# Order of a channel mixer's wide products, of the next weights' split and of two table transposes in a two-layer encoder trunk

## The chip, the cores and the metric

The kernel runs on one core of a Trainium2 chip. The metric is the device time of one execution in microseconds; the time before is the median of 3 runs. The profile is of one further execution.

The engines are named as in the profile: PE (TensorE's matmuls), PEld (its weight loads), DVE (VectorE), ACT (ScalarE), POOL (GpSimd) and SP (SyncE, which here only issues DMA).

## The reference, cut to what matters

The trunk has two layers over 512 tokens of width 1024. Each has a mixer and a channel mixer.

```python
h = rmsnorm(x, norm_mix_g[l])
proj = h @ a_w_in          # layer 0: queries, keys, values, output gate, 2*4 gate columns, memory queries
...
x = x + concat([mix_out, mem_out]) @ w_out

def conv_ffn(h, w_up, conv_w, conv_b, w_down):     # the channel mixer, D_FF = 2816
    u, g = split(h @ w_up, 2)
    g = causal_dwconv(g, conv_w, conv_b)           # width 3
    return (silu(g) * u) @ w_down
```

All is float32.

## The kernel before, in words

**Arithmetic.** A float32 operand is used as a pair of tiles: a high part, rounded to the type fp32r by ACT (`split`, line 118), and a low part, the remainder, which DVE subtracts (line 119). A product of two pairs is three matmuls (`mm3`, lines 162 to 164): high by high, high by low, low by high. All have 128 partitions and 128 stationary columns; what varies is the number of moving columns, mostly 512 (all tokens) or 256 (half of them). Here a matmul of 512 columns is called wide, one of 256 narrow. Weights come by DMA into `wr` and are split into `wh` and `wl`; each of the three has 3 buffers, the general scratch tile `t` has 8. PSUM tiles have the tags `mm` (3 buffers, `pmm` in the profile), `sc` (3, `psc`) and `tr` (2, `ptr`).

**The channel mixer.** For each of 22 tiles `j` of 128 hidden channels, an up tile and a gate tile are needed. Tiles 5 to 21 (`later`, line 780, one `step`, line 801, for each) take them together as a 2 by 2 block product (up and gate rows; two halves of the contraction; two halves of the tokens) with seven block products in place of eight. A block product of pairs is 12 narrow matmuls (4 contraction tiles by `mm3`; `products`, line 748). Three of the seven (`chain`, line 770, with the weights `s2`, `s3` and `a22`) are added onto the PSUM tile `r1`. In the 12 steps of each layer with `j` in `WIDE` (9 to 20) these three are made by `wide_products` (line 762): the moving tile holds a high part in its first 256 columns and the low part in the other 256, so for each of the 4 contraction tiles one wide matmul (line 767) with the high weights makes high by high and high by low, and one narrow one (line 768) with the low weights makes low by high in the first half. ACT (line 774) then copies the first half out and DVE (line 775) adds the other half.

Between them stand two blocks of the down projection (`down_products`, line 724): 4 contraction tiles by `mm3`, 12 wide matmuls each, into `ptr`. In a WIDE step PE's order is: 24 narrow (two products), the `s2` product, 12 wide (down block 0), 12 narrow, the `s3` product, 12 wide (down block 1), the `a22` product, 12 narrow. PE, ACT and DVE run in the order in which the code is written there (`manual_schedule`).

**The entry.** The first part of layer 0 (`value_columns(1)`, line 971) projects half of the value columns and the gate columns. It loops over 4 pairs of contraction tiles (`u`), each with one weight tile (392 columns) and 24 matmuls. The normalised input tiles are made at the same time: `x_scaled(j)` (DVE line 387, then ACT's cast line 392) and `x_low(j)` (DVE line 395). In the loop's pass `u` the kernel takes the weights that were split before, makes the input tiles `2u+2` and `2u+3`, and only then splits the weights of the next pass (`parts`, lines 118 and 119, pinned: kept in program order). Then come `load_vectors(1)` and `load_vectors(2)` (line 297): each loads a table of 88 rows by SP into a `t` tile (line 302), transposes it on PE into `ptr` (line 305) and copies it on DVE to a constant tile `cols` (line 307). They hold the convolution's coefficients of the two channel mixers. After that `value_columns(0)` and four projections with a convolution (`qk_tile`, line 1083; its accumulator is a `t` tile that ACT first writes at line 1088) and two gate tiles run on PE, woven with `gate_rows` (line 1012), a chain of small DVE and ACT operations that holds six more `t` tiles and sends rows out by DMA from POOL (line 1068, tensor `rowd`). Here a scheduler decides the order on each engine, with the pinned operations kept in theirs.

Of the kernel before, what the change touches and what calls it, by code (L numbers as in the profile page):

```python
# [45 lines left out]
H = S // 2  # L46
# [7 lines left out]
def trunk(  # L54
# [18 lines left out]
    nc = tc.nc  # L73
# [62 lines left out]
    def parts(raw, pinned=False):  # L136
        _, a, b = raw.shape
        hi = sb("wh", [P, D], F32R)[:, : a * b].rearrange("p (a b) -> p a b", a=a)
        lo = sb("wl", [P, D], F32R)[:, : a * b].rearrange("p (a b) -> p a b", a=a)
        split(hi, lo, raw, pinned=pinned)  # L140
        return hi, lo
# [36 lines left out]
    def run(gen):  # L178
        while True:
            try:  # L180
                next(gen)
            except StopIteration as end:
                return end.value

    def chain(*gens):
        for g in gens:
            yield from g
# [109 lines left out]
    def load_vectors(i, stage=None):  # L297
        n = sum(k for _, k in VECS[i])
        at = sum(k for group in VECS[:i] for _, k in group)
        if stage != 1:  # L300
            raw_vectors[i] = sb("t", [P, P])
            nc.sync.dma_start(raw_vectors[i][:n, :], vecs[at : at + n, :])
        if stage != 0:
            tp = ps("tr")
            nc.tensor.transpose(tp[:, :n], raw_vectors[i][:n, :], ident[:n, :n])
            cols = cpool.tile([P, n], F32, name=f"cols{i}")
            V.tensor_copy(cols, tp[:, :n])
            c = 0
            for name, k in VECS[i]:
                col[name] = cols[:, c : c + k]  # L310
                c += k
# [90 lines left out]
    def value_weights(hf, u):  # L402
        n = AW // 2
        ex = rows(a_w_in, 4 * AW, 2 * AH, 2 * u, 2 * u + 2) if hf else None
        return load(rows(a_w_in, 2 * AW + hf * n, n, 2 * u, 2 * u + 2), 2, n, ex)

    with tc.manual_schedule(engines={mybir.EngineType.PE, mybir.EngineType.Activation, mybir.EngineType.DVE}):

        w = ps("mm")
# [53 lines left out]
        vw = [parts(value_weights(1, 0))]  # L463
# [155 lines left out]
    class ChannelMixer:  # L619
# [139 lines left out]

            return [(p[i - 1][:, :H], p[i - 1][:, H:]) for p in self.sums]  # L760

        def wide_products(self, o, w, i):

            n = KT // 2
            for k in range(n):
                both = self.sums[k][i - 1]
                nc.tensor.matmul(o, w[0][:, k], both, start=False, stop=False, skip_group_check=True)  # L767
                nc.tensor.matmul(o[:, :H], w[1][:, k], both[:, :H], start=False, stop=k == n - 1, skip_group_check=True)  # L768

        def chain(self, to, o, w, i, wide):  # L770

            if wide:
                self.wide_products(o, w, i)
                A.copy(to, o[:, :H])  # L774
                V.tensor_tensor(out=to, in0=to, in1=o[:, H:], op=ALU.add)  # L775
            else:
                self.products(o, w, self.t(i))
                A.copy(to, o[:, :H])
# [22 lines left out]
        def step(self, j, w, nxt, tail):  # L801
            def then(o, *names):
                for name in names if o is not None else ():
                    getattr(o, name)()

            new = Tail(self, j)
            then(tail, "last_block", "first_tap")
            w.split_fourth()
            r1, r2, new.r3 = ps("mm"), ps("mm"), ps("sc")
            new.up, new.u3, new.pre = sb("t", [P, S]), sb("t", [P, S]), sb("t", [P, S])  # L810
            self.products(r1, w.a11, self.b(0, 0), True)
            A.copy(new.up[:, :H], r1[:, :H])
            then(tail, "second_tap")
            self.products(r2, w.a12, self.b(1, 0), True)
            V.tensor_tensor(out=new.up[:, :H], in0=new.up[:, :H], in1=r2[:, :H], op=ALU.add)
            then(tail, "third_tap")
            wide = j in WIDE
            self.chain(new.up[:, H:], r1, w.s2, 2, wide)
            then(nxt, "sums")
            then(tail, "gated")  # L820
            then(nxt, "split_second", "sum_third")
            w.down_products(0)
            self.products(new.r3, w.s1, self.t(1), True)
            w.add_down(0)
            then(tail, "split")
            then(nxt, "split_up")
            self.chain(new.u3[:, :H], r1, w.s3, 3, wide)
            V.tensor_tensor(out=new.pre[:, H:], in0=new.u3[:, :H], in1=new.r3[:, :H], op=ALU.add)
            then(nxt, "split_sums")
            w.down_products(1)  # L830
            then(nxt, "sum_fourth")
            w.add_down(1)
            self.chain(new.pre[:, :H], r1, w.a22, 4, wide)
            then(nxt, "split_down", "split_gate")
            self.products(new.r3, w.s4, self.b(1, 1))
            return new, nxt
# [134 lines left out]
    def value_columns(hf):  # L971
        n = AW // 2
        os_ = [ps(t) for t in ("mm", "mm", "mm", "sc")]
        for u in range(4):
            if hf:

                wh, wl = vw.pop()
                for j in range(2 * u + 2, min(2 * u + 4, KT)):
                    if j < KT - 1:
                        x_scaled(j + 1)  # L980
                    x_low(j)
                if u < 3:
                    vw.append(parts(value_weights(1, u + 1), pinned=True))
            else:
                wh, wl = parts(value_weights(0, u))
            nn = wh.shape[-1]
            for i in range(2):
                k = 2 * u + i
                for T in range(TT):
                    lh, ll = (t[:, T * P : (T + 1) * P] for t in act[k])  # L990
                    mm3(os_[T][:, :nn], lh, ll, wh[:, i, :], wl[:, i, :], k == 0, k == KT - 1)
                    yield
        for T in range(TT):
            if hf:
                V.tensor_add(gt[:, T, :], os_[T][:, n : n + 8], gateb)
            hi, lo = sb("u", [P, S], F32R), sb("u", [P, S], F32R)
            G.memset(f(hi)[:, DH : DH + P], 1.0)
            G.memset(f(lo)[:, DH : DH + P], 0.0)
            split(pair(hi), pair(lo), os_[T][:, :n].rearrange("p (a b) -> p a b", a=2))
            vh[hf][T], vl[hf][T] = hi, lo  # L1000
# [3 lines left out]
    e, u, c, r = (cpool.tile([P, TT, AH], F32, name=f"gate{i}") for i in range(4))  # L1004
# [224 lines left out]

    outp = OutProjection(a_w_out, mixes, (0, 3, "mm"), (3, 5, "sc"))  # L1230
    run(value_columns(1))
    load_vectors(1)
    load_vectors(2)
    for j in range(KT):
        pin(G.dma_start(xspill[j], xT[j]))
    fill = gate_rows()
    weave(chain(value_columns(0), a_tiles(0, 1)), fill, 0.3)
    run(fill)
    for s in range(TT):
        exponents(0, s)  # L1240
    for s in range(TT):
# [42 lines left out]
    for j in range(KT):  # L1284
        wh, wl = weights(rows(ffn_w_down[0], j * P, P, FT - LAST, FT), LAST, P)
        o = ps("mm")
# [174 lines left out]
    n = LAST // 2  # L1461
    for hf in range(2):
# [6 lines left out]
        for Ts, pieces in groups:  # L1469
            for c in pieces:  # L1470
                if c.start:
                    os_[Ts[0]] = ps("mm")
                for u in range(n):
# [3 lines left out]
                    wh, wl = ws[u]  # L1477
                    for T in Ts:
                        for i in range(2):
                            k = 2 * u + i  # L1480
# [58 lines left out]
```

## Time and profile before

| | us |
|---|---|
| median of 3 runs | 1193.16 (1192.63 to 1193.5) |
| the profiled execution, its own time | 1192.82 |
| its span | 1191.0 |
| PE busy | 1179.6 |
| DVE busy | 960.3 |
| ACT busy | 731.6 |

Matmuls are pipelined, so each one's duration in the trace (about 0.39 us wide, 0.28 us narrow) overlaps the next one's. What a matmul costs is the distance from its start to the next start, which the timeline shows. In the timeline a row is: start, duration, engine, line, operation, out<-in, shape, and in brackets the idle time before it and what ended it. For a matmul, `pmm<-u,wh` names the moving tile and then the stationary one or the other way round, as the kernel passes them.

### The profile page before, as it was taken

Reading aid. Unit: us, or ns where it says so; the run is one execution under the profiler, and the core shown is the slowest. Engines: PE = TensorE matmul, PEld = TensorE weight load, DVE = VectorE, ACT = ScalarE, POOL = GpSimd, SP = SyncE. Lnnn points to the kernel's source line nnn. Section 1 sums busy time; section 2 is a strip of 40 time slices with the busy share of each in tenths; the row PEclk is TensorE's granted clock in tenths of the full one; section 3 lists DMA queues with packets and bytes.
Section 4 is the critical chain, followed back from the end, with each engine's and each line's share of the span. In section 5 each row is a group of like instructions: output and inputs, shape, how many; then the busy total and the mean of one; then the engine's idle time right before and its main releaser. Section 6 shows DMA issues by size and latency. Waiting matters only on the chain.

```text
span 1191.0 us, 18093 instructions
## 1 busy us (share of the span) xinstructions
PE 1179.6 (99%) x6651; PEld 1029.0 (86%) x6651; DVE 960.3 (81%) x1720; ACT 731.6 (61%) x1299; POOL 145.7 (12%) x234
## 2 busy tenths in 40 slices
PE   9999999999999999999999999999999999999997
PEld 9988888888899889888888888888889988888986
DVE  6877788888878888888788888987896888888855
ACT  4547788766656555555576667775665655555545
POOL 0203102011021111101020000101101011111100
PEclk9999999999999999999999999999999999999999
DMA  8636422457475776665563223244746565665451
GB/s 280 203 107 154 105 75 71 140 172 171 97 174 139 166 165 159 162 141 116 157 214 106 80 71 96 71 135 152 185 100 131 135 138 127 141 142 141 118 158 71
DMA packets 208746, 162.80 MB, mean 137 GB/s; under 512 B 8484, under 2 KB 188170, under 8 KB 208658
## 3 DMA queue, kind: packets, MB, share of 16 engines
q1 hardware_dynamic: 186450, 120.78, 35.1%
q0 software_dynamic: 22208, 40.87, 17.4%
q8 instruction: 52, 0.85, 0.3%
q14 instruction: 36, 0.29, 0.1%
HBM read 133.09 MB, written 32.47 MB: 139 GB/s over the span
## 4 chain that ended last, share of the span: by engine, by line
PE 93%; DVE 3%; ACT 2%; issue 1%; DVEq 0%; ACTq 0%
PE pmm L162 15%; PE pmm L163 15%; PE pmm L164 15%; PE pmm L767 6%; PE ptr L162 6%; PE psc L164 6%; PE ptr L164 6%; PE psc L163 6%; PE ptr L163 6%; PE psc L162 6%; PE pmm L768 3%; PE psc L499 2%; PE ptr L1366 1%; PE ptr L1387 1%; PE ptr L1388 1%
## 5 line engine op out<-in xcount | busy, mean ns | idle before, releaser
L162 PE MATMUL pmm<-u,wh 128*128 128x512 f32 (+1 forms) x872 | 307.9, 353 | 0.1
L163 PE MATMUL pmm<-u,wh 128*128 128x512 f32 (+1 forms) x872 | 306.3, 351 | 0.5 <-DVE u L119 0.5
L164 PE MATMUL pmm<-u,wl 128*128 128x512 f32 (+1 forms) x872 | 306.2, 352 | 0.0
L119 DVE TENSOR_TENSOR wl<-wr,wh 128x1024 fp32r<-128x1024 f32 (+4 forms) x172 | 195.0, 1136 | 63.6 <-ACT wh L118 61.8
L118 ACT CAST wh<-wr 128x1024 fp32r<-128x1024 f32 (+4 forms) x172 | 168.4, 981 | 94.9 <-PE pmm L163 35.6
L164 PEld LDWEIGHTS pmm<-u,wl 128*128 128x128 f32 x872 | 165.1, 189 | 20.8
L163 PEld LDWEIGHTS pmm<-u,wh 128*128 128x128 f32 x872 | 165.4, 190 | 19.2 <-DVE u L119 1.1
L162 PEld LDWEIGHTS pmm<-u,wh 128*128 128x128 f32 x872 | 165.2, 190 | 18.7 <-ACT u L118 0.5
L735 POOL DMA_DIRECT2D xspill<-t x64 | 56.2, 878 | 398.7 <-ACT t L734 389.8
L162 PE MATMUL ptr<-u,wh 128*128 128x512 f32 x256 | 101.3, 396 | 0.0
L164 PE MATMUL ptr<-u,wl 128*128 128x512 f32 x256 | 100.4, 392 | 0.0
L163 PE MATMUL ptr<-u,wh 128*128 128x512 f32 x256 | 100.0, 391 | 0.0
L118 ACT CAST u<-pt 128x512 fp32r<-128x512 f32 x102 | 62.8, 618 | 45.9 <-DVE pt L865 45.8
L162 PE MATMUL psc<-u,wh 128*128 128x256 f32 (+1 forms) x248 | 82.4, 332 | 0.0
L163 PE MATMUL psc<-u,wh 128*128 128x256 f32 (+1 forms) x248 | 82.1, 331 | 0.0
L119 DVE TENSOR_TENSOR u<-pt,u 128x512 fp32r<-128x512 f32 x102 | 70.0, 687 | 5.8 <-ACT u L118 2.4
L928 ACT ACTIVATE t<-t 128x512 f32<-128x512 f32 x34 | 21.5, 633 | 78.9 <-DVE t L639 78.9
L767 PE MATMUL pmm<-u,u 128*128 128x512 f32 x192 | 69.7, 397 | 0.0
L775 DVE TENSOR_TENSOR t<-t,pmm 128x256 f32<-128x256 f32 x72 | 30.1, 418 | 47.2 <-ACT t L774 47.2
L734 ACT COPY t<-ptr 128x512 f32<-128x512 f32 x64 | 37.4, 585 | 45.0 <-PE ptr L164 45.0
L164 PE MATMUL psc<-u,wl 128*128 128x256 f32 (+1 forms) x200 | 63.5, 318 | 0.0
L639 DVE SCALAR_TENSOR_TENSOR t<-t,cols,t 128x511 f32<-128x511 f32 x80 | 59.5, 744 | 3.7 <-ACT t L646 3.7
(299 smaller groups left out, 2698.2 us busy)
## 6 DMA issues: line engine op xcount, KB each, us to landing
wr<-in_ffn_w_up_dram SPq DMA_DIRECT2D x54, 512.0 KB, 4.2
pt<-in_ffn_w_up_dram SPq DMA_DIRECT2D x34, 512.0 KB, 5.8
wr<-in_ffn_w_down_dram SPq DMA_DIRECT2D x34, 512.0 KB, 4.0
xspill<-t POOLq DMA_DIRECT2D x64, 256.0 KB, 5.0
wr<-in_a_w_in_dram SPq DMA_DIRECT2D x20, 512.0 KB, 3.8
xspill<-u POOLq DMA_DIRECT2D x32, 256.0 KB, 2.8
u<-xspill SPq DMA_DIRECT2D x32, 256.0 KB, 5.3
wr<-in_w_kv_dram SPq DMA_DIRECT2D x12, 512.0 KB, 3.7
```

The costliest lines, as they stand in the source:

```text
L118: high = A.copy(hi, src) if on_act else V.tensor_copy(hi, src)
L119: low = V.tensor_tensor(out=lo, in0=src, in1=f(hi), op=ALU.subtract)
L162: nc.tensor.matmul(o, lh, rh, start=first, stop=False, skip_group_check=more)
L163: nc.tensor.matmul(o, lh, rl, start=False, stop=False, skip_group_check=more)
L164: nc.tensor.matmul(o, ll, rh, start=False, stop=last, skip_group_check=more)
L499: nc.tensor.matmul(o, a, b, start=first and i == 0, stop=i == 1)
L639: V.scalar_tensor_tensor(acc[:, n:], src[:, : S - n], self.fw[:, c * FT + j : c * FT + j + 1], acc[:, n:], op0=ALU.mult, op1=ALU.add,)
L734: A.copy(t, o)
L735: G.dma_start(xspill[j], t, accum_op=ALU.add)
L767: nc.tensor.matmul(o, w[0][:, k], both, start=False, stop=False, skip_group_check=True)
L768: nc.tensor.matmul(o[:, :H], w[1][:, k], both[:, :H], start=False, stop=k == n - 1, skip_group_check=True)
L775: V.tensor_tensor(out=to, in0=to, in1=o[:, H:], op=ALU.add)
```

## The change

It has three parts.

1. In `wide_products` the eight matmuls of a product no longer alternate. Before down blocks 0 and 1 (`s2`, `s3`) the four narrow ones come first and the four wide ones after them, next to the block; in `a22`, behind down block 1, the four wide ones come first (`after=True`).
2. In `value_columns(1)` the split of the next pass's weights stands between the two input tiles of a pass, not behind both.
3. The two tables of `load_vectors` are loaded where they were, but transposed and copied only after the gate rows.

```diff
-        def wide_products(self, o, w, i):
+        def wide_products(self, o, w, i, after=False):
 
             n = KT // 2
-            for k in range(n):
-                both = self.sums[k][i - 1]
-                nc.tensor.matmul(o, w[0][:, k], both, start=False, stop=False, skip_group_check=True)
-                nc.tensor.matmul(o[:, :H], w[1][:, k], both[:, :H], start=False, stop=k == n - 1, skip_group_check=True)
-
-        def chain(self, to, o, w, i, wide):
+            halves = [p[i - 1] for p in self.sums]
+            jobs = [(o[:, :H], w[1][:, k], halves[k][:, :H]) for k in range(n)]
+            both = [(o, w[0][:, k], halves[k]) for k in range(n)]
+            jobs = both + jobs if after else jobs + both
+            for k, (to, lh, rh) in enumerate(jobs):
+                nc.tensor.matmul(to, lh, rh, start=False, stop=k == 2 * n - 1, skip_group_check=True)
+
+        def chain(self, to, o, w, i, wide, after=False):
 
             if wide:
-                self.wide_products(o, w, i)
+                self.wide_products(o, w, i, after)
...
-            self.chain(new.pre[:, :H], r1, w.a22, 4, wide)
+            self.chain(new.pre[:, :H], r1, w.a22, 4, wide, True)
...
         for u in range(4):
             if hf:
 
-                wh, wl = vw.pop()
+                wh, wl = vw.pop(0)
                 for j in range(2 * u + 2, min(2 * u + 4, KT)):
                     if j < KT - 1:
                         x_scaled(j + 1)
                     x_low(j)
-                if u < 3:
-                    vw.append(parts(value_weights(1, u + 1), pinned=True))
+                    if u < 3 and j == 2 * u + 2:
+                        vw.append(parts(value_weights(1, u + 1), pinned=True))
...
     run(value_columns(1))
-    load_vectors(1)
-    load_vectors(2)
+    load_vectors(1, 0)
+    load_vectors(2, 0)
...
     run(fill)
+    load_vectors(1, 1)
+    load_vectors(2, 1)
```

On PE, in a WIDE step, from the `s2` product to the first matmul of down block 0, before (the number behind a name is the tile's own; `u_3206`, `u_3260`, `u_3318` and `u_3372` are the moving tiles of the four contraction tiles, `u_4021` and `u_4022` the high and low weights):

```order
L767 MATMUL pmm_4129<-u_3206,u_4021 128x512
L768 MATMUL pmm_4129<-u_3206,u_4022 128x256
L767 MATMUL pmm_4129<-u_3260,u_4021 128x512
L768 MATMUL pmm_4129<-u_3260,u_4022 128x256
L767 MATMUL pmm_4129<-u_3318,u_4021 128x512
L768 MATMUL pmm_4129<-u_3318,u_4022 128x256
L767 MATMUL pmm_4129<-u_3372,u_4021 128x512
L768 MATMUL pmm_4129<-u_3372,u_4022 128x256
L162 MATMUL ptr_4182<-u_3382,wh_4094 128x512
```

The same place of the changed kernel, where the one call stands at line 770:

```order
L770 MATMUL pmm_4129<-u_3206,u_4022 128x256
L770 MATMUL pmm_4129<-u_3260,u_4022 128x256
L770 MATMUL pmm_4129<-u_3318,u_4022 128x256
L770 MATMUL pmm_4129<-u_3372,u_4022 128x256
L770 MATMUL pmm_4129<-u_3206,u_4021 128x512
L770 MATMUL pmm_4129<-u_3260,u_4021 128x512
L770 MATMUL pmm_4129<-u_3318,u_4021 128x512
L770 MATMUL pmm_4129<-u_3372,u_4021 128x512
L162 MATMUL ptr_4182<-u_3382,wh_4094 128x512
```

The same eight matmuls run, but the changes between 512 and 256 columns are fewer. The `s3` product moves in the same way; in `a22` the four wide ones follow down block 1 directly and the four narrow ones stand ahead of the 12 narrow ones of the step's last product. A WIDE step then has runs of 44 narrow (12 of the step before, 24, 4 of `a22` and 4 of `s2`), 16 wide, 16 narrow and 20 wide matmuls.

On DVE, in passes 0 and 1 of `value_columns(1)`, before (`wl_603` and `wl_646` are the low weights of passes 1 and 2, the rows of L387 and L395 the input tiles):

```order
L395 TENSOR_TENSOR u_537<-t_534,u_536 128x512
L387 SCALAR_TENSOR_TENSOR t_593<-u_454,cols_521,rb_517 128x512
L395 TENSOR_TENSOR u_590<-t_587,u_589 128x512
L119 TENSOR_TENSOR wl_603<-wr_599,wh_602 128x784
L387 SCALAR_TENSOR_TENSOR t_630<-u_461,cols_521,rb_517 128x512
L395 TENSOR_TENSOR u_596<-t_593,u_595 128x512
L387 SCALAR_TENSOR_TENSOR t_636<-u_468,cols_521,rb_517 128x512
L395 TENSOR_TENSOR u_633<-t_630,u_632 128x512
L119 TENSOR_TENSOR wl_646<-wr_642,wh_645 128x784
```

The same stretch of the changed kernel (`wl_597` and `wl_640` are the low weights of passes 1 and 2 there):

```order
L395 TENSOR_TENSOR u_537<-t_534,u_536 128x512
L119 TENSOR_TENSOR wl_597<-wr_593,wh_596 128x784
L387 SCALAR_TENSOR_TENSOR t_600<-u_454,cols_521,rb_517 128x512
L395 TENSOR_TENSOR u_590<-t_587,u_589 128x512
L387 SCALAR_TENSOR_TENSOR t_630<-u_461,cols_521,rb_517 128x512
L395 TENSOR_TENSOR u_603<-t_600,u_602 128x512
L119 TENSOR_TENSOR wl_640<-wr_636,wh_639 128x784
L387 SCALAR_TENSOR_TENSOR t_643<-u_468,cols_521,rb_517 128x512
L395 TENSOR_TENSOR u_633<-t_630,u_632 128x512
```

Each weight split has moved two rows forward, past one L387 and one L395. On ACT the cast of the high weights has moved ahead of one cast of an input tile in the same way (`wh_596` now follows `u_589` directly).

On PE, in the last pass of `value_columns(1)`, the changed kernel (`wh_682` and `wl_683` are that pass's weights, `psc_778` and `wh_781` belong to `value_columns(0)`, which follows):

```order
L162 MATMUL pmm_583<-wh_682,u_645 128x392
L162 MATMUL pmm_584<-wh_682,u_645 128x392
L162 MATMUL pmm_585<-wh_682,u_645 128x392
L162 MATMUL psc_586<-wh_682,u_645 128x392
L162 MATMUL psc_778<-wh_781,u_525 128x384
L163 MATMUL pmm_583<-wl_683,u_645 128x392
L164 MATMUL pmm_583<-wh_682,u_646 128x392
```

Before, the scheduler had put no matmul of `value_columns(0)` ahead of the end of `value_columns(1)`; now one matmul with the next weights stands 20 rows ahead of it. Behind the pass the two matmuls of line 305 stood before; they now follow the last matmul of the two gate tiles.

## The prediction

> **What bounds the kernel now.** I read the page first, for the share of each engine and the granted clock.
>
> ```profile
> span 1191.0 us, 18093 instructions
> PE 1179.6 (99%) x6651; PEld 1029.0 (86%) x6651; DVE 960.3 (81%) x1720; ACT 731.6 (61%) x1299; POOL 145.7 (12%) x234
> PEclk9999999999999999999999999999999999999999
> PE 93%; DVE 3%; ACT 2%; issue 1%; DVEq 0%; ACTq 0%
> ```
>
> PE is busy all the time at an even clock and carries 93% of the chain that ended last. So time comes only from PE: a wait of PE that goes, or matmuls that start closer together. The view of PE's waits, its longest row:
>
> ```profile
> PE pmm L162 <- ACT wh L118: 1.4, 1, 1.4
> ```
>
> It is one wait of 1.4 us in a span of 1191. What else is to be had stands in the distance between starts, and that I read from PE's timeline. First, wide matmuls in a long run without narrow ones (layer 0's channel mixer, before the WIDE steps), and then one block of 12 wide ones that stands between long runs of narrow ones, with the first WIDE step behind 48 narrow ones:
>
> ```profile
> 299.51 0.39 PE L164 MATMUL psc<-u,pt 128*128 128x512 f32 x1
> 299.74 0.39 PE L162 MATMUL psc<-u,wh 128*128 128x512 f32 x1
> 299.96 0.39 PE L163 MATMUL psc<-u,wh 128*128 128x512 f32 x1
> 300.19 0.39 PE L164 MATMUL psc<-u,pt 128*128 128x512 f32 x1
> ...
> 382.11 0.40 PE L162 MATMUL ptr<-u,wh 128*128 128x512 f32 x1
> ...
> 384.86 0.28 PE L162 MATMUL pmm<-u,u 128*128 128x256 f32 x1
> ```
>
> The long run takes 0.68 us for three, 0.227 us a wide matmul. The block of 12 takes 384.86 - 382.11 = 2.75 us, 0.03 us more than 12 x 0.227 = 2.72: that is what one entry from narrow to wide costs when clean runs meet. Now one WIDE step, from its `s2` product to the next one's:
>
> ```profile
> 390.61 0.40 PE L767 MATMUL pmm<-u,u 128*128 128x512 f32 x1
> ...
> 396.24 0.40 PE L767 MATMUL pmm<-u,wh 128*128 128x512 f32 x1
> ...
> 397.65 0.40 PE L162 MATMUL ptr<-u,wh 128*128 128x512 f32 x1
> ...
> 400.43 0.39 PE L767 MATMUL pmm<-u,u 128*128 128x512 f32 x1
> ...
> 401.83 0.28 PE L162 MATMUL psc<-u,u 128*128 128x256 f32 x1
> ...
> 406.15 0.40 PE L767 MATMUL pmm<-u,u 128*128 128x512 f32 x1
> ```
>
> The step takes 406.15 - 390.61 = 15.54 us, with no idle bracket in it. The 48 narrow ones from 384.86 to 390.61 give 5.75 / 48 = 0.120 us a narrow matmul. By these two paces the `s3` product (396.24 to 397.65, four of each) would take 4 x (0.227 + 0.120) = 1.39; it takes 1.41. The block behind it (to 400.43) takes 2.78 in place of 2.72. So where 512 and 256 columns alternate, the starts are a little further apart, and the block behind them pays too.
>
> **Part 1, the wide products.** Nothing is added or removed on any engine; the order on PE changes, and the runs become 44 narrow, 16 wide, 16 narrow, 20 wide: 60 narrow x 0.1198 = 7.19 us, 36 wide x 0.2267 = 8.16, and two entries of 0.03: 15.41 us. Against 15.54 that is 0.13 us a step. How many steps:
>
> ```profile
> L767 PE MATMUL pmm<-u,u 128*128 128x512 f32 x192 | 69.7, 397 | 0.0
> L767 PE MATMUL pmm<-u,wh 128*128 128x512 f32 x96 | 34.9, 398 | 0.0
> ```
>
> 192 + 96 = 288 wide matmuls at 12 a step are 24 steps: 24 x 0.13 = 3.1 us. The bounds: with no cost at all for an entry 15.35, 0.19 a step, 4.6 us; if each of the two entries keeps what the block behind an alternation pays now (2.78 - 2.72 = 0.06), 15.47, 0.07 a step, 1.7 us. I take the middle one, since its row is a block of the same tiles between clean runs.
>
> Here a rule of the Trainium skill speaks against the change. The trace has 0.227 us and 0.120 us in clean runs and 2.78 us for a block whose clean price is 2.72. The page "TensorE: Matmul & The Clock Gate", section "Back-to-back issue gap", gives the distance of warm matmuls as the moving columns over 2.4 GHz plus 2.5 ns, by the number of columns alone, whatever stands before. By it this part would be worth nothing, since the same matmuls run. Worked out as an estimate it gives 0.216 and 0.109 us; the trace doesn't agree, in both paces and in that the same 12 matmuls take 2.75 or 2.78.
>
> What hides the change from the other engines: each product ends as far ahead of the next block as before, as the last wide one starts 0.23 us ahead of it and lasts 0.40, where the last narrow one starts 0.12 ahead and lasts 0.28. The first matmul of `a22` writes `r1`, which ACT and DVE must have read after `s3`:
>
> ```profile
> 397.85 0.37 ACT L774 COPY t<-pmm 128x256 f32<-128x256 f32 x1 [0.22 <-PE pmm L768]
> 398.80 0.41 DVE L775 TENSOR_TENSOR t<-t,pmm 128x256 f32<-128x256 f32 x1
> ```
>
> DVE has read it at 399.21, and `a22` starts at 400.43: 1.22 us to spare, of which the shorter block takes some 0.05.
>
> **Part 2, the weights' split at the entry.** Here PE, ACT, DVE and SP around the wait of 1.44 us:
>
> ```profile
> 40.19 0.34 PE L164 MATMUL pmm<-wh,u 128*128 128x392 f32 x1
> 41.96 0.80 PE L162 MATMUL pmm<-wh,u 128*128 128x392 f32 x3 [1.44 <-ACT wh L118]
> ...
> 52.92 0.34 PE L164 MATMUL psc<-wh,u 128*128 128x392 f32 x1
> ...
> 55.05 0.34 PE L164 MATMUL psc<-wh,u 128*128 128x392 f32 x1
> 55.23 0.32 PE L305 MATMUL ptr<-ident,t 88*128 88x88 f32 x2
> 55.34 0.42 PE L162 MATMUL pmm<-wh,u 128*128 128x384 f32 x1
> ```
>
> ```profile
> 37.36 1.28 ACT L392 CAST u<-t 128x512 fp32r<-128x512 f32 x2 [0.76 <-DVE t L387]
> 40.55 0.62 ACT L392 CAST u<-t 128x512 fp32r<-128x512 f32 x1 [1.90 <-DVE t L387]
> 41.07 0.84 ACT L118 CAST wh<-wr 128x784 fp32r<-128x784 f32 x1
> ```
>
> ```profile
> 39.17 0.68 DVE L395 TENSOR_TENSOR u<-t,u 128x512 fp32r<-128x512 f32 x1
> 39.77 0.74 DVE L387 SCALAR_TENSOR_TENSOR t<-u,cols,rb 128x512 f32<-128x512 f32 x1
> 40.43 0.68 DVE L395 TENSOR_TENSOR u<-t,u 128x512 fp32r<-128x512 f32 x1
> 41.94 0.97 DVE L119 TENSOR_TENSOR wl<-wr,wh 128x784 fp32r<-128x784 f32 x1 [0.83 <-ACT wh L118]
> ```
>
> ```profile
> 29.38 0.37 SPq L131 DMA_DIRECT2D wr<-in_a_w_in_dram x1
> 42.95 0.37 SPq L131 DMA_DIRECT2D wr<-in_a_w_in_dram x1
> wr<-in_a_w_in_dram SPq DMA_DIRECT2D x7, 384.0 KB, 4.6
> ```
>
> PE needs pass 1's high weights at 40.19 + 0.18 = 40.37 and gets them at 41.96, because ACT's cast at 41.07 stands behind the cast at 40.55, and that behind DVE's L387 at 39.77. In the new order ACT can cast them behind the two casts of 37.36, from 38.6 to 39.4; they were issued at 29.38, and the median transfer takes 4.6 us. DVE takes the low part at 39.77, done at 40.7; PE needs it four matmuls into the pass, at 41.1. The wait goes: 41.96 - 40.37 = 1.59 us.
>
> After the wait the 72 matmuls of passes 1 to 3 take 55.23 - 41.96 = 13.27 us. Their pace at the end is (55.05 - 52.92) / 12 = 0.1775, which would make 12.78; 0.49 us go to small gaps behind the wait, with the low weights arriving late. So the most that this part can bring is 1.59 + 0.49 = 2.1 us (2.3 with the rounding of the steps). What is late next: the input tiles, which the split now stands ahead of. I rolled DVE and ACT on with the starts above (L387 0.66 to the next, L395 0.60, the split 0.90 to 0.97, and between them the wait for ACT's cast). DVE then ends the low weights of passes 2 and 3 at about 45.1 and 49.4, and PE, with 24 x 0.1775 = 4.26 us a pass, needs them at 45.3 and 49.7; the second input tile of pass 1 is needed at 42.8 and ready at 42.1. All are met, with 0.2 to 0.7 us to spare. I take 2.1 us; if the two short margins fail by half a microsecond each, 1.1 us are left.
>
> The matmul with `wh_781` that now stands 20 rows ahead of the end of the last pass is a new wait, behind which all of PE's matmuls queue. Its weights are asked for when DVE has split pass 1's (before: 41.94 + 0.97, and SP at 42.95; now about 40.75), land 4.6 us later at 45.4 and are cast behind pass 3's at about 49.2. PE gets there at 49.6.
>
> **Part 3, the tables.** The two transposes take 55.34 - 55.23 = 0.11 us where they are and as much where they go, so they cost nothing; the two copies on DVE move too, and no step of PE waits for them. What is new is that two of the eight `t` tiles stay taken while the gate rows hold six. By the order's list of waits, the second convolution's accumulator on ACT now waits for the first two `rowd` transfers, whose tile it takes over:
>
> ```profile
> 82.70 0.52 POOL L1068 DMA_DIRECT2D rowd<-t  x1 [5.22 <-DVE t L1066]
> rowd<-t POOLq DMA_DIRECT2D x1, 6.0 KB, 1.7
> 85.10 0.76 ACT L1088 ACTIVATE t<-pmm,cols 128x512 f32<-128x512 f32 x1
> ```
>
> The second transfer lands at 84.4, 0.7 us ahead of ACT's step at 85.10, and all of this moves forward together with PE. Behind that step ACT queues casts of weights that PE uses microseconds later. I take nothing, and up to 0.2 us either way.
>
> **The sum.** 3.1 + 2.1 = 5.2 us. The profiled execution took 1192.82, which becomes 1187.6. The median of the runs shown is 0.34 above it: 1188.0.
>
> **The rivals.** First, order doesn't matter: the distances in the alternation come from something that stays (the tiles of the product, or PSUM). Then only the entry pays: 1193.16 - 2.1 = 1191.1. Against it speaks that a block of 12 wide ones, the same in both places, takes 2.75 behind narrow ones and 2.78 behind an alternation. The rule of the Trainium skill's page "TensorE: Matmul & The Clock Gate" named above would end here. Second, the entry gives nothing: another weight or input tile is as late as the one repaired, and PE waits as long a little later: 1193.16 - 3.1 = 1190.1. For it speaks that the margins above are 0.2 to 0.7 us and worked out by hand. Third, slower: the matmul with `wh_781` blocks PE. It is the only place where the change puts a wait in front of work that could run. Each microsecond by which its cast ends after 49.6 costs one; after 5.2 all that was won is gone, and after 7.6 the kernel is 2.4 us slower, 1195.6. The transfer would then have to take some 15 us where the median takes 4.6.
>
> **How the numbers follow.** A measurement of this kernel can tell about 0.2%, 2.4 us, from no change; faster therefore means below 1190.8. The forecast, both parts with their bounds, has a chance of 0.80; the entry giving nothing 0.08, which is still faster; order not mattering 0.09, which counts as the same; the blocked PE 0.03. So faster 0.88, the same 0.09, slower 0.03. The range takes the bounds: 4.6 + 2.3 = 6.9 below 1193.16 is 1186.3, and 1.7 + 1.1 = 2.8 below it is 1190.4. It holds the second rival and leaves out the first and the third.
>
> **What would show it.** A WIDE step of 15.41 us from `s2` to `s2` in place of 15.54, and blocks of 12 between wide ones in place of the alternation at 0.227 us each, show part 1; a step of 15.54 refutes it. No idle bracket of PE near 40.4 and the matmul that stands at 55.34 now starting near 53.2 show part 2. A bracket on the matmul of `value_columns(0)` near 49.6, on ACT's L1090 near 83, or on the first matmul of `a22`, would show the waits that I hold to be covered. A time above 1190.4 or below 1186.3 would show a price that I have not seen.

## The result, and the profile after

| | before | after |
|---|---|---|
| median of the runs taken together on one chip | 1193.51 us (1192.63 to 1195.81, 6 runs) | 1188.69 us (1188.06 to 1190.78, 6 runs) |
| ratio, 95% interval | | 0.9961, 0.9949 to 0.9973 |
| the profiled execution and its span | 1192.82 us, 1191.0 us | 1188.06 us, 1186.1 us |

The changed kernel is 4.8 us faster; the interval holds 3.2 to 6.1 us. The forecast was 1188.0 with a range of 1186.3 to 1190.4. One of the seven executions of an experiment below (the wide products alone) took 1943.39 us at a granted clock of 0.56, and its ratio leaves that one out. The page of the changed kernel begins like this (span, busy time of the engines, granted clock, chain of waits by engine):

```profile
span 1186.1 us, 18067 instructions
PE 1175.6 (99%) x6651; PEld 1030.1 (87%) x6651; DVE 960.2 (81%) x1720; ACT 731.5 (62%) x1299; POOL 144.6 (12%) x234
PEclk9999999999999999999999999999999999999999
PE 94%; DVE 2%; ACT 2%; issue 1%; DMA 0%; ACTq 0%; DVEq 0%
```

PE still bounds all, with the same number of matmuls. One WIDE step of the changed kernel on PE's timeline, where the view joins matmuls of one line into groups (x8 is four of 256 columns and four of 512):

```profile
389.31 1.57 PE L770 MATMUL pmm<-u,u 128*128 128x256 f32 x8
...
394.87 0.64 PE L770 MATMUL pmm<-u,wl 128*128 128x256 f32 x4
395.35 1.09 PE L770 MATMUL pmm<-u,wh 128*128 128x512 f32 x4
...
399.01 1.54 PE L770 MATMUL pmm<-u,u 128*128 128x512 f32 x8
...
404.71 1.57 PE L770 MATMUL pmm<-u,u 128*128 128x256 f32 x8
```

From `s2` to `s2` it is 404.71 - 389.31 = 15.40 us, where it was 15.54. Now the entry, first PE at the old wait and at the end of the last value pass, with the matmul with `wh_781` as the second of the row at 49.53, and then ACT's step near 83 that the prediction named:

```profile
40.29 0.34 PE L164 MATMUL pmm<-wh,u 128*128 128x392 f32 x1
40.47 0.69 PE L162 MATMUL pmm<-wh,u 128*128 128x392 f32 x3
...
49.53 0.51 PE L162 MATMUL psc<-wh,u 128*128 128x392 f32 x2
...
53.25 0.34 PE L164 MATMUL psc<-wh,u 128*128 128x392 f32 x1
54.26 0.41 PE L162 MATMUL pmm<-wh,u 128*128 128x384 f32 x1 [0.67 <-DVE gt L997]
```

```profile
83.77 0.76 ACT L1090 ACTIVATE t<-pmm,cols 128x512 f32<-128x512 f32 x1
```

The wait of 1.44 us at 40.4 is gone, and the two rows that might have become waits carry no bracket. But the next product's first matmul, which could have started at 53.25 + 0.18 = 53.43, starts at 54.26, behind a wait that the kernel before doesn't have. What holds it is seen on SP, ACT and DVE:

```profile
40.86 4.71 SPq L131 DMA_DIRECT2D wr<-in_a_w_in_dram  x2
```

```profile
51.10 0.84 ACT L118 CAST wh<-wr 128x768 fp32r<-128x768 f32 x1 [1.87 <-DMA wr<-in_a_w_in_dram]
53.04 0.86 ACT L118 CAST u<-pmm 128x384 fp32r<-128x384 f32 x2 [1.10 <-DVE gt L997]
```

```profile
48.53 1.84 DVE L119 TENSOR_TENSOR wl<-wr,wh 128x784 fp32r<-128x784 f32 x2
51.98 0.96 DVE L119 TENSOR_TENSOR wl<-wr,wh 128x768 fp32r<-128x768 f32 x1 [1.60 <-ACT wh L118]
52.85 0.23 DVE L997 TENSOR_TENSOR gt<-pmm,gateb 128x8 f32<-128x8 f32 x2
53.56 0.56 DVE L119 TENSOR_TENSOR u<-pmm,u 128x384 fp32r<-128x384 f32 x1 [0.47 <-ACT u L118]
```

Read it from below. PE's `pmm` bank is free when DVE has taken the low part of the first eviction (53.56 + 0.56 = 54.12; the bracket of PE names the gate addition, of which one ends at about the same time). That needs ACT's cast at 53.04, that the gate addition at 52.85, and this stands in DVE's order behind the split of 51.98. The split is of the second next weights: the second of SP's pair, issued at about 45.2 and landed by 51.1, when ACT casts them. DVE waits 1.60 us for weights that PE uses only near 57.6, while a bank that PE uses at 53.43 is kept full.

Where the 4.9 us between the last matmuls of the two profiled executions lie, counted by the k-th matmul of each on PE (differences to the kernel before in us, minus where it is earlier; the entry is the stretch from 22 to 108 us, which holds the tables' two transposes in either place, and its first half ends at 45 us; the WIDE steps are all 24, elsewhere is the rest). Below this count is called the ledger:

| kernel | first 22 us | entry, its first half and second half | WIDE steps | elsewhere | all |
|---|---|---|---|---|---|
| after | +0.10 | -2.01 +0.81 | -3.36 | -0.49 | -4.94 |
| after, measured again | 0.00 | -2.00 +0.67 | -3.36 | +0.41 | -4.28 |

So the entry gives 2.0 us and loses 0.7 to 0.8 of it again. What lies elsewhere is mostly not the change's: it is 0.49 us less in one profile and 0.41 us more in the other of the same kernel.

### The profile page after: what moved, and what is told of

It is laid out like the page before. It is cut to its first block, busy times and chain, and to the rows that moved or that the text cites. A ratio compares the mean times of both kernels' runs of the same rounds, so it can differ in the third digit from the quotient of the medians.

```text
span 1186.1 us, 18067 instructions
## 1 busy us (share of the span) xinstructions
PE 1175.6 (99%) x6651; PEld 1030.1 (87%) x6651; DVE 960.2 (81%) x1720; ACT 731.5 (62%) x1299; POOL 144.6 (12%) x234
## 4 chain that ended last, share of the span: by engine, by line
PE 94%; DVE 2%; ACT 2%; issue 1%; DMA 0%; ACTq 0%; DVEq 0%
PE pmm L162 15%; PE pmm L164 15%; PE pmm L163 15%; PE pmm L770 8%; PE ptr L162 6%; PE ptr L163 6%; PE ptr L164 5%; PE psc L164 5%; PE psc L163 5%; PE psc L162 5%; PE psc L499 2%; PE ptr L1370 1%; PE ptr L582 1%; PE ptr L1391 1%; PE ptr L1392 1%; PE ptr L568 1%
## 5 line engine op out<-in xcount | busy, mean ns | idle before, releaser
L770 PE MATMUL pmm<-u,u 128*128 128x256 f32 (+1 forms) x384 | 74.7, 337 | 0.0
L770 PEld LDWEIGHTS pmm<-u,u 128*128 128x128 f32 x384 | 60.7, 190 | 7.8
```

The costliest lines, as they stand in the source:

```text
L770: nc.tensor.matmul(to, lh, rh, start=False, stop=k == 2 * n - 1, skip_group_check=True)
```

## The experiments

The first four kernels were timed together. Three leave parts of the change out, one turns the grouping round.

**The wide products alone** (the kernel before, with the new `wide_products`, `chain` and the call for `a22`):

> The kernel before with the grouped wide products alone. Theory (each switch from 256 to 512 columns costs PE time, and grouping leaves 2 of 13 switches a step): a WIDE step takes 15.40 us from `s2` to `s2` in place of 15.54, 24 x 0.14 = 3.4 us, so the time is 3.2 to 3.6 us below the kernel before. The wait of 1.4 us near 40.4 us stays. Rival (the gain after the change came from the entry and from chance, and order doesn't matter): within 0.5 us of the kernel before.

1190.06 us against 1192.90 for the kernel before, 2.8 us less by the medians; ratio 0.9971, 0.9959 to 0.9983, which is 3.5 us less, between 2.0 and 4.9. In the ledger the WIDE steps give 3.36 us and all of it 3.31; the old wait stands (PE's longest wait):

```profile
PE pmm L162 <- ACT wh L118: 1.4, 1, 1.4
```

Order matters, and the prediction's first rival falls.

**The entry alone** (the kernel before with the split and the tables, WIDE steps as before):

> The kernel before with the weights' split at the entry and the tables alone; WIDE steps as before. Theory (the wait near 40.4 us goes, but the second next weights land late, hold DVE ahead of the gate additions and so PE for 0.7 to 0.9 us near 54): 1.0 to 1.5 us below the kernel before, with a bracket of about 0.7 us on the first matmul of the next product near 54.3 us. Rival, the prediction's sum: 2.1 us below and no such bracket. In both a WIDE step stays at 15.54 us.

1192.99 us, ratio 0.9996, 0.9987 to 1.0005: between 1.6 us less and 0.6 more, which can't be told from nothing. The 1.0 to 1.5 us that I had expected are not seen in the time. PE at the start of the next product:

```profile
55.52 0.34 PE L164 MATMUL psc<-wh,u 128*128 128x392 f32 x1
56.68 0.41 PE L162 MATMUL pmm<-wh,u 128*128 128x384 f32 x1 [0.82 <-DVE gt L995]
```

The bracket is there, as expected. In the ledger its entry gives 2.00 us and loses 0.98, net 1.02. That the profiled execution is none the less slower than the kernel before (1194.47) comes from another place, long before the first instruction that the change moves:

```profile
7.11 1.11 PE L422 MATMUL psc<-ident,u 128*128 128x128 f32 x4 [0.98 <-DMA u<-in_mem_dram]
```

PE waits here for the first loads, and behind it matmuls of 256 columns start 0.21 us apart until 10.4 us, although the granted clock reads 1.00 there. Other profiles wait 1.1 and 1.2 us at the same place and go on at the usual pace; what slows this one isn't shown. The first 22 us of this profile are 2.36 us longer than before's; over all profiles they vary from -0.27 to +2.36. The entry's gain of 1.02 us is smaller than this variation.

**Grouped, but on the far side** (the changed kernel with one line turned round):

```diff
-            jobs = both + jobs if after else jobs + both
+            jobs = jobs + both if after else both + jobs
```

> The changed kernel with the wide products still grouped, but on the far side: ahead of the narrow ones in `s2` and `s3`, behind them in `a22`. A step then enters 5 runs of wide matmuls in place of 2 (13 before). Theory (an entry behind a long narrow run costs 0.02 to 0.026 us net): 15.46 to 15.48 us a step, 1.4 to 1.9 us above the changed kernel. Rival 1 (each of the 11 switches saved is worth the same 0.013 us): 15.44 us, 0.9 us above. Rival 2 (only the strict alternation costs, the neighbour block doesn't matter): 15.40 us, the same time as the changed kernel.

1190.91 us, ratio 0.9982, 0.9973 to 0.9991. One step from `s2` to `s2` on PE's timeline:

```profile
390.42 1.56 PE L770 MATMUL pmm<-u,u 128*128 128x512 f32 x8
...
405.89 1.56 PE L770 MATMUL pmm<-u,u 128*128 128x512 f32 x8
```

15.47 us, as the theory of the price of an entry had it; the WIDE steps give 1.60 us where the changed kernel's give 3.36. Of these two orders, standing together alone brings half of the gain, and standing beside the block as well brings the other half.

**The split without the tables' move** (against the entry alone):

```diff
-    load_vectors(1, 0)
-    load_vectors(2, 0)
+    load_vectors(1)
+    load_vectors(2)
...
-    load_vectors(1, 1)
-    load_vectors(2, 1)
```

> The kernel before with the weights' split at the entry, and the two tables where they stood, in front of the next product. Theory (the tables cost nothing in either place): within 0.2 us of the kernel with entry and tables. Rival: the tables' transposes and copies stand between the last value product and the next on PE and DVE, just where the evictions are late now, and add 0.1 to 0.5 us.

1194.72 us, ratio 1.0014, 1.0005 to 1.0022, single runs from 1192.73 to 1197.56: slower than the kernel before, and 1.7 us above the entry alone, more than either theory had. PE, and then the busy time, the granted clock (the column behind POOL's) and the busy share of the DMA engines (behind the clock) in stretches:

```profile
49.87 0.34 PE L162 MATMUL psc<-wh,u 128*128 128x392 f32 x1
53.02 0.58 PE L305 MATMUL ptr<-ident,t 88*128 88x88 f32 x2 [2.81 <-DMA t<-in_vecs_dram]
53.32 0.68 PE L163 MATMUL pmm<-wl,u 128*128 128x392 f32 x1
53.79 0.53 PE L164 MATMUL pmm<-wh,u 128*128 128x392 f32 x1
54.12 0.53 PE L163 MATMUL pmm<-wl,u 128*128 128x392 f32 x1
```

```profile
49.00:50.00 1.00, 1.00 (x7) 0.88 (x5) 1.00 (x2) 0.57 (x1) 0.00 (x0) 1.00 1.02 362
50.00:53.00 3.00, 0.21 (x2) 0.01 (x1) 0.72 (x1) 0.83 (x1) 0.00 (x0) 0.88 1.00 332
53.00:54.00 1.00, 0.98 (x4) 0.98 (x5) 0.56 (x3) 0.00 (x0) 0.00 (x0) 0.50 0.86 315
...
58.00:59.00 1.00, 1.00 (x4) 1.00 (x4) 0.64 (x3) 0.48 (x1) 0.00 (x0) 0.50 0.01 1
59.00:60.00 1.00, 1.00 (x7) 1.00 (x7) 0.79 (x4) 0.16 (x1) 0.00 (x0) 0.95 0.00 0
```

The tables aren't where they stood. With the new split, the scheduler puts their two transposes into the last value pass, 20 matmuls ahead of its end, where their transfer isn't there yet: PE waits 2.81 us. Then the clock is granted at 0.50 for 6 us, and matmuls that started 0.178 us apart start 0.328 apart (54.12 - 53.79 = 0.33): 16 of them at 0.15 more and one at 0.30 make 2.7 us. The ledger has 5.83 us lost behind the old wait.

**The changed kernel again, and three repairs of the new wait**, timed together.

> The changed kernel once more, on a chip together with the next three. Theory (the two parts simply add, and the entry nets 0.3 to 1.1 us of its 2 us): 3.4 + 0.7 = 4.1 us below the kernel before, 3.7 to 4.6. Rival (the parts help each other beyond their sum, or the first measurement's 4.8 us is the steady value): 4.8 us or more.

1188.67 us (1188.29 to 1189.58), ratio 0.9963, 0.9951 to 0.9976: 4.7 us less by the medians. That lies between the two theories, and the interval holds both, so the timing doesn't decide. The ledger (above) speaks for the sum of the two parts: the WIDE steps give the same 3.36 us here as alone, and the entry 1.33, a little more than the 1.1 that I had allowed; 0.41 us are lost elsewhere.

The writes of `xspill` later:

```diff
-    for j in range(KT):
-        pin(G.dma_start(xspill[j], xT[j]))
     fill = gate_rows()
-    weave(chain(value_columns(0), a_tiles(0, 1)), fill, 0.3)
+
+    def spills():
+        for j in range(KT):
+            pin(G.dma_start(xspill[j], xT[j]))
+        yield from ()
+
+    weave(chain(value_columns(0), spills(), a_tiles(0, 1)), fill, 0.3)
```

> The changed kernel with the eight writes of `xspill` issued behind the next value product, not ahead of it. Theory (these writes share the DMA with the second next weights, whose late landing holds DVE ahead of the gate additions): the weights land about 4 us after their issue at 45.2, near 49.5 and not 51.1, the bracket on the first matmul of the next product (0.7 us) goes, and the time is 0.8 us below the changed kernel. Rival (the chain of addition, cast and subtraction behind the last value matmul is itself too long): the bracket stays at 0.3 us or more, and the gain is under 0.4 us.

1189.17 us (1188.35 to 1189.36), ratio 0.9963, 0.995 to 0.9977: no gain in the time. ACT's cast of the second weights, and PE at the start of the next product:

```profile
51.52 0.84 ACT L118 CAST wh<-wr 128x768 fp32r<-128x768 f32 x1 [1.21 <-DMA wr<-in_a_w_in_dram]
```

```profile
54.32 0.34 PE L164 MATMUL psc<-wh,u 128*128 128x392 f32 x1
54.68 0.41 PE L162 MATMUL pmm<-wh,u 128*128 128x384 f32 x1
```

The weights land 2.80 us ahead of the last value matmul (54.32 - 51.52), where the changed kernel has 53.25 - 51.10 = 2.15: 0.65 us earlier, not the 1.6 that I had expected. The 0.65 are enough to shrink the wait from 54.26 - 53.43 = 0.83 to 54.68 - 54.50 = 0.18. But the edit did less than its text says. POOL's issues of the writes, first in the changed kernel and then here:

```profile
41.87 4.26 POOL L1237 DMA_DIRECT2D xspill<-u  x8
```

```profile
44.14 4.28 POOL L1240 DMA_DIRECT2D xspill<-u  x8
```

The first 22 us of this profile are 1.07 us longer, so the scheduler issues the writes only 1.2 us later (44.14 - 41.87 - 1.07), still around the second weights' issue and not behind the next value product. What the transfer would take without them is not shown. In the ledger the entry is 1.82 us below the kernel before, 0.5 to 0.6 better than the changed kernel's, and the first 22 us of this profile give 1.16 back.

The evictions ahead of the second weights:

```diff
-                wh, wl = parts(value_weights(0, u))
+                wh, wl = vn.pop(0) if vn else parts(value_weights(0, u))
...
+        if hf:
+            vn.append(parts(value_weights(0, 0)))
         for T in range(TT):
+            if hf and T == 3:
+                vn.append(parts(value_weights(0, 1), pinned=True))
             if hf:
-                V.tensor_add(gt[:, T, :], os_[T][:, n : n + 8], gateb)
+                pin(V.tensor_add(gt[:, T, :], os_[T][:, n : n + 8], gateb))
...
-            split(pair(hi), pair(lo), os_[T][:, :n].rearrange("p (a b) -> p a b", a=2))
+            split(pair(hi), pair(lo), os_[T][:, :n].rearrange("p (a b) -> p a b", a=2), pinned=hf == 1)
```

> The changed kernel with the second next weights split behind the first three evictions on ACT and DVE, in program order, and the writes of `xspill` where they are, so that the late landing stays but holds nothing. Theory (the wait is one of order in DVE's queue): the transfer still lands near 51, the bracket near 54.3 goes, 0.8 us below the changed kernel. Rival (the evictions are themselves the limit, or the second weights are then late for PE near 57.6): the bracket stays, or a new one stands near 57.6; gain under 0.4 us or a loss.

1188.26 us (1188.10 to 1188.47), ratio 0.9958, 0.9946 to 0.9971. ACT and PE:

```profile
54.75 0.48 ACT L118 CAST u<-pmm 128x384 fp32r<-128x384 f32 x1 [0.70 <-DVE gt L1003]
55.13 1.57 ACT L118 CAST wh<-wr 128x768 fp32r<-128x768 f32 x2
```

```profile
53.42 0.34 PE L164 MATMUL psc<-wh,u 128*128 128x392 f32 x1
53.62 0.41 PE L162 MATMUL pmm<-wh,u 128*128 128x384 f32 x1
```

The transfer and the writes are untouched, the second weights are cast 4 us later than in the changed kernel, and the wait is gone. This is the clean test: it was the order in DVE's queue. (The edit changes ACT's order too, but in the changed kernel ACT stood idle for 1.10 us ahead of its first eviction, waiting for DVE.) In the ledger the entry gives 1.84 us net, 0.5 to 0.6 more than the changed kernel's. By the times it is 0.4 us, which is inside both spreads.

Both edits together:

> Both edits: the writes later, and the three evictions ahead of the second weights. Theory: either edit alone takes the whole wait, so both together are worth 0.8 us, not 1.6, and the spread from run to run is smaller than the changed kernel's. Rival (each takes a part of it): more than either alone by 0.3 us or more.

1188.22 us (1187.36 to 1189.47), ratio 0.9958, 0.9946 to 0.9971; the entry gives 1.83 net, the same as either edit alone. They remove the same wait. The spread, which I had expected to shrink, didn't; the first 22 us of this profile alone take 1.18 us more than before's.

**Three more**, on the steps that were still open. The wide products in twos:

```diff
-            jobs = both + jobs if after else jobs + both
+            first, second = (both, jobs) if after else (jobs, both)
+            jobs = first[:2] + second[:2] + first[2:] + second[2:]
```

> The changed kernel with the wide products in twos: two narrow, two wide, two narrow, two wide in `s2` and `s3`, and in `a22` two wide, two narrow, two wide, two narrow. A step enters 5 runs of wide matmuls, as many as on the far side, but three of them behind only two narrow ones. Theory A (an entry has one price, 0.025 us, however long the narrow run): 15.35 + 5 x 0.025 = 15.47 us a step. Theory B (an entry costs less behind a short narrow run; behind a single narrow one, as in the kernel before, (15.54 - 15.35 - 2 x 0.025) / 11 = 0.013 us): 15.44 to 15.46 us. Theory C (the entries aren't what costs, the number of narrow matmuls that lie next to a wide one is): above the far side's 15.47.

1188.51 us (1188.08 to 1189.50), ratio 0.996, 0.9945 to 0.9974. One step:

```profile
390.20 1.56 PE L771 MATMUL pmm<-u,u 128*128 128x256 f32 x8
...
405.57 1.56 PE L771 MATMUL pmm<-u,u 128*128 128x256 f32 x8
```

15.37 us: below the changed kernel's 15.40, so all three theories are refuted, mine of a price for each entry among them. The distances between starts in ns, as medians over 22 steps (w behind a distance that follows a matmul of 512 columns), show why. The first row is the end of the changed kernel's `s2` and the block behind it, the second the same with twos, the third the kernel before:

```
after   120 120 120 120 233w 236w 228w 233w 231w 226w 227w 227w ... 227w 113 119 120
twos    120 120 233w 236w 116 112 232w 231w 227w 227w 227w 227w ... 227w 113 119 120
before  233w 118 241w 120 236w 113 232w 118 241w 237w 234w 235w 224w 230w 236w 229w ... 226w 114 119 120
```

Each switch starts a ripple that lasts six matmuls or more: wide ones come late, the first narrow ones behind them early. Against 227 and 120, four wide behind narrow ones pay 0.022 us and the block behind them 0.004. Two pay 0.015 and get 0.012 back on the two narrow ones that follow, the next two pay 0.009, and the block nothing. In the alternation the narrow ones give back less than the wide ones pay, 0.023 us over the product, and the block of 12 behind it pays another 0.059.

The tables' move alone, on the kernel before:

> The kernel before with the two tables' transposes behind the gates alone. Theory (they run 0.11 us on PE in either place, and in the kernel before their transfer has landed 3 us ahead): within 0.3 us of the kernel before. Rival (they hold something there too): 1 us or more below it.

1193.21 us (1192.35 to 1195.60), ratio 0.9999, 0.999 to 1.0009. In the kernel before, the place of the tables makes no difference that the time shows, within about 1.1 us. The ledger shows a small loss by the move: 0.11 us in the entry, and 0.33 us near 123 us, where PE multiplies `pt` and `u` tiles into `ptr`. All ten profiles of kernels with the tables moved lose 0.04 to 0.52 us in this place, the changed kernel's two 0.07 and 0.50; the three of kernels that don't move them lose nothing. What holds PE there isn't shown.

The split without the tables' move, with the writes of `xspill` later:

> The kernel with the split and the tables where they stood, whose two transposes the scheduler puts into the last value pass, 20 rows ahead of its end, but with the writes of `xspill` issued behind the next value product. Theory (PE's wait of 2.8 us there, and the half clock behind it, come from the tables' transfer, which shares the DMA with these writes): the wait shrinks to 0 to 1.5 us, the clock stays at 1.00, and the time falls by 1 to 5 us against the same kernel with the writes early, to 1190.5 to 1193. Rival (the tables are late because SP issues them behind two weights, whatever the writes do): the wait and the half clock stay, 1194 to 1196.

1195.91 us (1193.59 to 1198.15), ratio 1.0023, 1.0012 to 1.0034.

```profile
49.16 0.34 PE L162 MATMUL psc<-wh,u 128*128 128x392 f32 x1
52.19 0.89 PE L305 MATMUL ptr<-ident,t 88*128 88x88 f32 x2 [2.68 <-DMA t<-in_vecs_dram]
```

The wait stays at 2.68 us, and the half clock with it, as the rival had it. But the cause stays open. Here too the writes are issued only 1.2 us later (at 42.69, where the split without this edit has 42.22 and first 22 us that are 0.69 longer), still ahead of the tables at 45.26; and while PE waited for the tables without this edit, the DMA engines were fully busy (1.00 in the stretch from 50 to 53). So the runs don't tell SP's order from the shared DMA.

**Both improvements in one kernel**, twos and evictions first:

> The changed kernel with the wide products in twos and the first three evictions ahead of the second weights. Theory (the two gains lie on PE in different places and add): a WIDE step of 15.37 us, 24 x 0.03 = 0.7 us, and no bracket near 54.3, 0.6 us; together 1.3 us below the changed kernel, 1187.0 to 1187.6. Rival (the pairs' step was an accident of that program's alignment and is 15.40 again): 0.6 us below the changed kernel.

1186.85 us (1186.52 to 1187.70), ratio 0.9946, 0.9932 to 0.9959, against 1192.76 for the kernel before on that chip. PE in one step, and at the next product:

```profile
389.04 1.56 PE L771 MATMUL pmm<-u,u 128*128 128x256 f32 x8
...
404.41 1.56 PE L771 MATMUL pmm<-u,u 128*128 128x256 f32 x8
```

```profile
53.43 0.34 PE L164 MATMUL psc<-wh,u 128*128 128x392 f32 x1
53.62 0.41 PE L162 MATMUL pmm<-wh,u 128*128 128x384 f32 x1
```

15.37 us a step and no wait. In the ledger the WIDE steps give 4.16 us and the entry 1.84. This is 5.9 us below the kernel before of its own group, where the changed kernel was 4.8 and 4.7 below: 1.1 to 1.2 us more, and 1.3 to 1.5 in the ledger's two parts. The theory had 1.3. (The changed kernel was not timed in this group, and the 1186.85 itself lies just below the range that I had given.)

## Why the prediction was right, and where it was not

**Part 1, the wide products, was right in direction and nearly in size; its mechanism only in part.** The forecast was 15.41 us a step and 3.1 us in all; the trace has 15.40 and 3.36, and the kernel with this part alone the same 3.36 in its WIDE steps. The 0.26 us between come from a step that went from 15.540 to 15.400, 0.14 where 0.13 was taken. That order matters, and that the block behind an alternation pays, came out. The two entries of 0.03 were measured at 0.027 each over the 16 and 20 wide matmuls, less 0.006 that the narrow ones behind give back. What doesn't hold is one price for each entry: five entries to a step took 15.47 us on the far side and 15.37 in twos, the latter less than the changed kernel's two. That the price read from one block fitted the changed kernel is because there, too, long runs meet.

The page "TensorE: Matmul & The Clock Gate" of the Trainium skill, section "Back-to-back issue gap", gives the distance by a formula in the columns alone and says that in a stream the weight loads set it too; the order of the widths stands in neither. The traces don't agree: the same 36 wide and 60 narrow matmuls, each with a 128x128 weight, take 15.54, 15.47, 15.40 and 15.37 us in four orders.

**Part 2, the entry, was mis-sized: 2.1 us forecast, 0.8 to 1.3 in the ledgers of five profiles.** The step that failed is "All are met, with 0.2 to 0.7 us to spare. I take 2.1 us". What the prediction had rolled forward came out: DVE's low weights of pass 3 stand at 48.53 as the first of two and are done at about 49.4 (forecast 49.4), the matmul with `wh_781` starts unhindered at 49.71 (forecast 49.6), and by then PE is 2.1 us ahead of the kernel before. The list of what is late next was too short. It held the input tiles and the first of the next weights, not the second, whose split stands in DVE's order ahead of the gate additions and the evictions. In the kernel before, the same order held nothing up: DVE's first low part there is

```profile
54.59 0.56 DVE L119 TENSOR_TENSOR u<-pmm,u 128x384 fp32r<-128x384 f32 x1
```

and ends at 55.15, while PE was busy up to the product's first matmul at 55.34. The evictions put first brought the term to 1.84 us; of the rest, 0.15 us is lost in that stretch even with the entry unchanged (the wide products alone). The prediction's second rival, that another wait takes the place of the one removed, was therefore partly true, and the entry alone can't be told from no change by its time.

**Part 3, the tables, was put at nothing as a move on its own, and the time agrees** (ratio 0.9999); the wait on ACT near 83 didn't come. The ledger has a small loss that the prediction lacked, 0.04 to 0.52 us near 123 us, often more than the 0.2 it allowed. And that the transposes cost nothing where they are holds for the kernel before only. With the split they no longer stay there: the scheduler draws them forward, and without the move they cost 4.9 us in the profile (the entry loses 3.84 us there and gains 1.02 with the move). Part 3 is what makes part 2 possible. The diff doesn't tell that; an order of part 2 without part 3 would have.

**The third rival, PE blocked**, didn't happen in the changed kernel. The split without the tables' move shows such a block in another place, and that its price of one microsecond for each of waiting was too low: 2.81 us of waiting brought 2.7 more through the clock.

**The sum** was 5.2; in the ledger the changed kernel's parts make 3.36 + 1.2 to 1.3 = 4.6 to 4.7, and the medians 4.7 and 4.8 with more than a microsecond of uncertainty. Part 1 brought 0.26 us more than forecast and part 2 0.8 to 0.9 less; that the two misses offset each other in part is luck. The forecast missed the median by 0.7 us, half of which is the kernel before, whose median in this group is 0.35 us higher. The rest of a profile varies from run to run by more than that: -0.27 to +2.36 us in the first 22 us and -0.49 to +0.47 elsewhere.

## What to carry to other kernels

When a wait on the bounding engine is taken away, roll the next product's loads and evictions forward too, in the order of each in-order engine: whatever waits for a transfer and stands ahead of an eviction can become the next wait. A term that depends on a scheduler is to be tried part by part, since a part that costs nothing alone may be what keeps another part cheap; and whether an edit moved what it was to move is read from the trace, as two of these moved their writes by 1.2 us only. Matmuls of different widths should be grouped where they meet a run of their own width, and small groups are worth a try: the distance of starts depends on the neighbours, and it is measured in one step of a trace.

## What the runs showed of the hardware

- A wait of 2.81 us (and one of 2.68) lowered PE's granted clock to 0.50. The mean of 0.88 over 50 to 53 us makes 0.72 us at half, so the clock fell near 52.3, 2.1 us after PE had gone idle at 49.87 + 0.34 = 50.21. The mean of 0.95 over 59 to 60 us puts the way back near 59.1, after 6.1 us of dense matmuls. The wait of 1.44 us in the kernel before left it at full. The page "TensorE: Matmul & The Clock Gate" of the Trainium skill, section "What's actually happening", names an idle window of about 3.4 us and as long a busy one for the way back. Here less idle time was enough, and the way back took longer.
- With 128x128 weights, wide matmuls in clean runs start 227 ns apart and narrow ones 120. Behind a switch the distances ripple for six matmuls or more, 224 to 241 and 112 to 121. What in PE makes the ripple, these runs don't show.
- PE's start depends on the first loads: the matmul behind the first 150 started between 21.8 and 24.4 us in fourteen profiles of kernels that are the same up to there.
